# Other fixed sums, a different split of the gather work and an earlier load of v in the expert stage of a decoder layer

## The chip, the core and the metric

The kernel runs on one core of a Trainium2 chip. The metric is device time in microseconds (us), from the start of the program to its end, lower is better. The core's engines each work through their own queue of instructions in a fixed order: TensorE (PE in the profile; PEld is its weight load), VectorE (DVE), ScalarE (ACT), GpSimd (POOL) and SyncE (SP). SP issues most of the transfers; POOL issues the gathers. An instruction whose inputs or buffer aren't ready holds up everything behind it on its engine.

## The reference, cut to what matters

```python
# x: 1024 tokens x 1024; two norm/mix layers come first, then PEER:
q = (xb @ w_query).reshape(T, 8, 2, 128)
s = einsum('thpk,hpnk->thpn', q, sub_keys)        # 8 heads, 2 x 128 keys
...                                               # top 16 of 16 x 16 pairs per head
idx = ...                                         # 128 of 16384 experts for each token
gate = softmax(best_s)
u, v = expert_u[idx], expert_v[idx]               # rows of 1024
act = gelu(einsum('td,thkd->thk', xb, u))
out = einsum('thk,thkd->td', gate * act, v)
```

Each token uses 128 of 16384 experts. The kernel computes this in two ways. For 352 tokens it gathers the 128 rows of u and the 128 rows of v that a token names (the gather way). For the other 672 tokens it multiplies with all 16384 experts, densely, and weighs the result with a gate matrix that is zero where an expert was not chosen (the dense way).

## The kernel before

The change concerns the last stage alone, from about 1260 us to the end. It walks over 128 blocks of 128 experts. All matrix products are done with split operands: an f32 matrix is kept as a high half (name ending in h) and a remainder (l), and a product is three matmuls, high by high, high by remainder, remainder by high. A split is an ACT copy to the high half (line 115) and a DVE subtraction for the remainder (line 116).

For each block `b`:

- `u_steps(b)` (line 1155) is the **first product**: the block's u (`wh`, `wl`, fetched as `in_uT` by SP at line 203) times the 672 dense tokens, in two column parts of 384 and 288 (`SPL`), 24 matmuls each, into two PSUM banks named `pa`. A Gelu on ACT (line 1168) empties each bank into a tile `Wl`. For 40 blocks (`EARLIES`, every third one) this was done in an earlier stage; the result is loaded from memory instead (`Wl<-ged`, line 1450).
- `w_step(b)` (line 1382) multiplies by the gates on DVE (line 1384) and splits the result into `Wh`, `Wl`.
- `v_load(b)` (line 1387) loads the block's v (`vl<-in_v`, line 1389) and splits it into `vh`, `vl`.

After every third block `v_phase` (line 1392) does the **second product** of three earlier blocks: for each of the two column parts j and each of the eight slices c of the 1024 output columns, nine matmuls (3 blocks by 3). There are 16 such sums per phase. Twelve go to a PSUM bank, alternately `pa` (the two banks that the first product also uses) and `pv` (two more), and DVE then adds them to `acc` tiles (line 1419). Four of them, the pairs (j, c) in `FIXED`, have a bank of their own (`pacc`) for the whole stage and are not added up in between.

One **group** of work is therefore: two first products (call them u A and u B), one loaded block, and one phase; 96 + 144 = 240 matmuls. The phase that follows u B works on the blocks up to u A, so u B's result is not needed at once.

The gather way runs beside it, as background work: POOL issues one gather of 128 rows per step (line 1084, five row buffers), DVE multiplies and sums u rows (line 1102) or adds v rows (line 1094). `along(columns)` releases as many background steps as the matmul columns just issued have earned. The order of instructions on each engine is then settled by a scheduler when the kernel is built: it ranks instructions by their place in the program and moves up what it holds to be ready.

Of the kernel before, what the change touches and what calls it, by code (L numbers as in the profile page):

```python
# [19 lines left out]
P = 128  # L20
S = 1024
DM = 1024
# [8 lines left out]
NK = 128  # L31
# [19 lines left out]
EARLY = 40  # L51
EARLIES = [b for b in range(NK) if b % 3 == 1][:EARLY]
SLOTS = SB + 1
ROWS = 4
TB = 8
NE = 3.6
NF = 2.1 * TG / 64
MID = 1
WL = 3
WS = SLOTS + 2  # L60
VS = SLOTS + 2
WB = 2
WJ = 0
PAIRS = [(0, 2), (2, 4)]
FIXED = [(0, 1), (0, 5), (1, 1), (1, 5)]
RB = 0.15
RD = 0.0
DG = 2
# [31 lines left out]
def build(tc, A, out, dbg=None):  # L100
    nc = tc.nc
    V, C, G, T, SY = nc.vector, nc.scalar, nc.gpsimd, nc.tensor, nc.sync
    dbg = dbg or {}

    def pool(st, name, bufs=1, side="left", space=None):
        kw = {} if space is None else {"space": space}
        if space is DRAM:
            return st.enter_context(tc.tile_pool(name=name, bufs=bufs, **kw))
        if space is PSUM:
            return st.enter_context(tc.tile_pool(name=name, bufs=bufs, reuse_waits="tile", **kw))  # L110
        return st.enter_context(tc.tile_pool(name=name, bufs=bufs, side=side, reuse_waits="tile", **kw))

    def split(hi, lo, src):

        C.activation(hi, src, AF.Copy)  # L115
        V.tensor_tensor(lo, src, hi.bitcast(F32), op=OP.subtract)  # L116

    def raw_tile(pl, shape, name, lb):

        return pl.tile(shape, F32R, name=name + "l", bufs=lb).bitcast(F32)  # L120

    def halves_of(pl, raw, shape, name, lb, hb):
        hi = pl.tile(shape, F32R, name=name + "h", bufs=hb)
        lo = pl.tile(shape, F32R, name=name + "l", bufs=lb)
        split(hi, lo, raw)
        return hi, lo
# [15 lines left out]
    with root:  # L142
# [29 lines left out]
        def advance(cost):  # L172
            if bg["back"] is None:
                return
            bg["due"] += cost
            while bg["spent"] < bg["due"]:
                bg["spent"] += next(bg["back"], 1e9)
# [826 lines left out]
        def norm_store(pl, o, w, parts, fw, r, sq):  # L1004

            sf = pl.tile([P, 4], F32, name="sf", bufs=3)[:w]
            for j in range(2):
                C.activation(sq[:w], parts[j], AF.Square, accum_out=sf[:, j:j + 1])
            V.scalar_tensor_tensor(sf[:, 0:1], sf[:, 0:1], DM * EPS, sf[:, 1:2], op0=OP.add, op1=OP.add)
            rsqrt(sf[:, 2:3], sf[:, 0:1], sf[:, 3:4], 5)  # L1010
            for j in range(2):
                sl = slice(j * 512, j * 512 + 512)
                V.scalar_tensor_tensor(r[:w, sl], parts[j], sf[:, 2:3], fw[:w, sl], op0=OP.mult, op1=OP.mult)
            SY.dma_start(out[o:o + w], r[:w])
# [165 lines left out]
        def u_early(blocks, rate):  # L1180

            left = blocks * 3.0 * KC * TD
            while left > 0:
                c = next(early, None)
                if c is None:
                    return False
                left -= c
                advance(c / 2400.0 * RATES[rate])
            return True
# [33 lines left out]
        def early_along(steps_):  # L1223
            for c in steps_:
                fill[0] += c * NE / 26.0
                if fill[0] - fill[1] > 0.25:
# [16 lines left out]
        for g in range(FULL, NG):  # L1243
            o, w = GG[g]
            r = slice(P - REST + o, P - REST + o + w)
            n = steps[g]
# [42 lines left out]
        def gates(t):  # L1289
# [3 lines left out]
            for q4 in range(w // TG):  # L1293
# [17 lines left out]
                for qb in range(TG // TB):  # L1311
# [24 lines left out]
                    advance(TB * 0.107 * RATES["F"])  # L1336
                    u_early(NF * TB / TG, "F")
                SY.dma_start(gd[:, :, (t * P) // TG + q4].rearrange("g p b t -> p g b t"),
# [4 lines left out]
        while u_early(1.0, "G"):  # L1343
# [5 lines left out]
        mp = pool(stM, "mp")  # L1349
        psM = pool(stM, "psM", space=PSUM)  # L1350
        accs = {(j, c): mp.tile([P, n], F32, name=f"acc{j}{c}") for j, (_, n) in enumerate(SPL) for c in range(KC)
                if (j, c) not in FIXED}
        fixed = {f: psM.tile([P, 512], F32, name=f"pacc{f[0]}{f[1]}", bufs=1) for f in FIXED}

        turn = [0]

        def new_pv():

            turn[0] ^= 1
            if turn[0]:  # L1360
                return psU.tile([P, 512], F32, name="pa", bufs=2)
            return psM.tile([P, 512], F32, name="pv", bufs=2)
# [8 lines left out]
        def along(columns):  # L1371
            advance(columns * per_column)
# [3 lines left out]
        Vs = {}  # L1376

        def g_load(q):
            gs[q] = mp.tile([P, NTG, GB, TG], F32, name="gsb", bufs=2)
            SY.dma_start(gs[q], gd[q])  # L1380
# [4 lines left out]
            Ws[b] = halves_of(mp, ge, [P, TD], "W", WS, SLOTS)  # L1385

        def v_load(b):
            raw = raw_tile(mp, [P, DM], "v", VS)
            SY.dma_start(raw, A["v"][b * P:(b + 1) * P])
            Vs[b] = halves_of(mp, raw, [P, DM], "v", VS, SLOTS)  # L1390

        def v_phase(b0, b1):
            last = b1 == NK
            for j, (o, n) in enumerate(SPL):
                for c in range(KC):
                    fx = (j, c) in fixed
                    pv = fixed[j, c] if fx else new_pv()
                    i = 0
                    for b in range(b0, b1):
                        wh, wl = Ws[b]  # L1400
                        vh, vl = Vs[b]
                        for l, r in ((vh, wh), (vl, wh), (vh, wl)):
                            T.matmul(pv[:, :n], l[:, c * P:(c + 1) * P], r[:, o:o + n],  # L1403
                                     start=(i == 0 and (not fx or b0 == 0)),
                                     stop=(i == 3 * (b1 - b0) - 1 and (not fx or last)))
                            i += 1
                    if last and fx:
                        accs[j, c] = raw_tile(mp, [P, TD], "W", WS)[:, :n]
                    a = accs.get((j, c))
                    if last and fx:  # L1410
                        C.activation(a, pv[:, :n], AF.Copy, scale=modc[:, 5, c:c + 1])
                    elif last:
                        V.scalar_tensor_tensor(a, pv[:, :n], modc[:, 5, c:c + 1], a, op0=OP.mult, op1=OP.add)
                    elif fx:
                        pass
                    elif b0 == 0:
                        V.tensor_copy(a, pv[:, :n])
                    else:
                        V.tensor_tensor(a, a, pv[:, :n], op=OP.add)  # L1419
                    if not last:  # L1420
                        along(3.0 * (b1 - b0) * n)
                if last:
                    for t in range(o // P, -(-(o + n) // P)):
                        w = WT[t]
                        parts = []
                        for q in range(2):
                            pt = new_pv()[:w]
                            for c in range(4):
                                cs_ = slice((q * 4 + c) * P, (q * 4 + c + 1) * P)
                                d = pt[:, c * P:(c + 1) * P]  # L1430
                                if j:
                                    T.matmul(d, ident[:w, :w], x1s[t][:w, cs_], start=True, stop=False)
                                    T.matmul(d, accs[j, q * 4 + c][:, t * P - o:t * P - o + w], ident, start=False, stop=True)
                                else:
                                    T.transpose(d, accs[j, q * 4 + c][:, t * P - o:t * P - o + w], ident)
                            if j == 0:
                                sl = slice(q * 512, (q + 1) * 512)
                                V.tensor_tensor(rs[t][:w, sl], pt, x1s[t][:w, sl], op=OP.add)
                                pt = rs[t][:w, sl]
                            parts.append(pt)  # L1440
                        norm_store(mp, REST + t * P, w, parts, fw, rs[t], sq)
# [3 lines left out]
        for b in range(NK):  # L1445
            if b % GB == 0 and b + GB < NK:
                g_load(b // GB + 1)
            if b in EARLIES:
                ge = raw_tile(mp, [P, TD], "W", WS)
                SY.dma_start(ge, ged[EARLIES.index(b)])  # L1450
            else:
                ge = raw_tile(mp, [P, TD], "W", WS)
                for c in u_steps(b, ge):
                    along(c)
            w_step(b, ge)
            v_load(b)
            if b - prev == SB:
                v_phase(prev, prev + SB)
                prev += SB
        for _ in bg["back"] or ():  # L1460
            pass
        while NK - prev > SB:
            v_phase(prev, prev + SB)
            prev += SB
# [5 lines left out]
        for t in range(DT):  # L1470
            n = ("wl", "wh")[t % 2] if t < 5 else "vl"
# [69 lines left out]
```

## Time and profile before

| | |
|---|---|
| median of 3 runs | 2999.6 us (2998.78 to 3002.16) |
| the profiled execution | 2986.61 us, span 2984.8 us |
| mean granted TensorE clock | 0.981 of full speed |
| PE busy / DVE busy over the span | 95% / 85% |
| ACT busy / POOL busy over the span | 31% / 29% |
| the stage that is changed | about 1260 to 2964 us |

Busy shares are unions of the recorded instructions. "Idle before" an instruction is put down to what released it. A wait on PE counts only while nothing runs on it; the first matmuls after a wait can also be slower.

### The profile page before, as it was taken

How to read it: one execution, taken by the hardware profiler on the slowest of the kernel's cores; microseconds unless marked ns; L12 is line 12 of the kernel's file. 1: busy time of each engine (PE TensorE's matmuls, PEld its weight loads, DVE VectorE, ACT ScalarE, POOL GpSimd, SP SyncE). 2: the span in 40 equal slices, each digit the busy share in tenths (PEclk: the TensorE clock that was granted, in tenths of full speed). 3: DMA queues.
4: the chain of work that ended last, by engine and by line, in shares of the span. 5: the costliest groups of instructions: out<-in, count | busy, mean ns of one | idle time of the engine just before them, and what ended most of it. 6: DMA issues, size and time to landing. Idle time of an engine off the chain costs nothing.

```text
span 2984.8 us, 47174 instructions
## 1 busy us (share of the span) xinstructions
PE 2850.0 (95%) x18190; PEld 2687.0 (90%) x18190; DVE 2547.3 (85%) x5369; ACT 939.3 (31%) x1548; POOL 862.6 (29%) x726
## 2 busy tenths in 40 slices
PE   8999999989999999999999999999899999899998
PEld 6887898878999889999999999999899999899998
DVE  6885549988999987488999989889899988899998
ACT  5643645333222455422222222222222222222222
POOL 0000000000000000045554544445454554555451
PEclk9999999989999999999999999999999999999999
DMA  7424342244223687788889989899899998899995
GB/s 271 146 90 140 127 155 64 78 141 146 70 90 112 212 253 244 246 307 323 324 324 330 340 321 340 325 323 332 304 351 327 329 324 316 311 327 329 324 320 182
DMA packets 288676, 740.01 MB, mean 248 GB/s; under 512 B 27873, under 2 KB 122081, under 8 KB 282050
## 3 DMA queue, kind: packets, MB, share of 16 engines
q0 software_dynamic: 102944, 374.78, 35.3%
q1 hardware_dynamic: 185506, 362.22, 35.3%
q8 instruction: 142, 2.33, 0.3%
q14 instruction: 84, 0.69, 0.1%
HBM read 666.29 MB, written 70.52 MB: 247 GB/s over the span
## 4 chain that ended last, share of the span: by engine, by line
issue 27%; DVE 25%; DMA 20%; PE 20%; POOL 5%; ACT 2%; SPq 0%; DVEq 0%; POOLq 0%; ACTq 0%
PE pp L469 5%; DVE gacc L1094 5%; DMA wl<-in_uT 3%; DVE wl L116 3%; DVE acc L1419 3%; DMA Wl<-ged 2%; PE pq L875 2%; PE pp L875 2%; DVE vl L116 2%; DVE Wl L1384 1%; DMA more<-in_u,idx 1%; PE pa L1163 1%; PE ps L579 1%; PE pp L380 1%; POOL more L1084 1%
## 5 line engine op out<-in xcount | busy, mean ns | idle before, releaser
L1163 PE MATMUL pa<-h2h,wh 128*128 128x384 f32 (+1 forms) x1840 | 590.3, 321 | 14.2 <-DVE acc L1419 12.0
L1163 PE MATMUL pa<-h2l,wh 128*128 128x384 f32 (+1 forms) x1840 | 588.0, 320 | 0.0
L1163 PE MATMUL pa<-h2h,wl 128*128 128x384 f32 (+1 forms) x1840 | 584.0, 317 | 2.7 <-DVE wl L116 2.7
L1163 PEld LDWEIGHTS pa<-h2h,wh 128*128 128x128 f32 x1840 | 347.9, 189 | 19.4 <-DVE acc L1419 13.3
L1163 PEld LDWEIGHTS pa<-h2h,wl 128*128 128x128 f32 x1840 | 349.0, 190 | 2.9 <-DVE wl L116 2.9
L1163 PEld LDWEIGHTS pa<-h2l,wh 128*128 128x128 f32 x1840 | 349.7, 190 | 0.0
L115 ACT ACTIVATE Wh<-Wl 128x672 fp32r<-128x672 f32 x128 | 98.0, 766 | 754.4 <-PE pv L1403 487.9
L115 ACT ACTIVATE wh<-wl 128x1024 fp32r<-128x1024 f32 x187 | 197.7, 1057 | 385.6 <-DMA wl<-in_uT 187.1
L1403 PE MATMUL pa<-Wh,vh 128*128 128x384 f32 (+1 forms) x768 | 251.5, 327 | 53.6 <-ACT Wl L1168 41.7
L116 DVE TENSOR_TENSOR wl<-wl,wh 128x1024 fp32r<-128x1024 f32 x187 | 228.0, 1219 | 75.3 <-ACT wh L115 74.6
L1403 PE MATMUL pv<-Wh,vh 128*128 128x384 f32 (+1 forms) x768 | 245.4, 320 | 5.2 <-DVE acc L1419 4.9
L1403 PE MATMUL pa<-Wl,vh 128*128 128x384 f32 (+1 forms) x768 | 245.8, 320 | 0.7 <-DVE Wl L116 0.7
L1403 PE MATMUL pa<-Wh,vl 128*128 128x384 f32 (+1 forms) x768 | 245.6, 320 | 0.0
L1403 PE MATMUL pv<-Wh,vl 128*128 128x384 f32 (+1 forms) x768 | 243.7, 317 | 0.0
L1403 PE MATMUL pv<-Wl,vh 128*128 128x384 f32 (+1 forms) x768 | 243.3, 317 | 0.0
L1403 PEld LDWEIGHTS pa<-Wh,vh 128*128 128x128 f32 x768 | 145.7, 190 | 67.7 <-ACT Wl L1168 52.1
L115 ACT ACTIVATE vh<-vl 128x1024 fp32r<-128x1024 f32 x128 | 134.4, 1050 | 125.5 <-DMA vl<-in_v 75.5
L1403 PE MATMUL pacc<-Wh,vh 128*128 128x384 f32 (+1 forms) x512 | 163.6, 320 | 1.5 <-ACT vh L115 1.5
L1403 PE MATMUL pacc<-Wh,vl 128*128 128x384 f32 (+1 forms) x512 | 163.7, 320 | 0.6 <-DVE vl L116 0.6
L1403 PE MATMUL pacc<-Wl,vh 128*128 128x384 f32 (+1 forms) x512 | 163.0, 318 | 0.0
L116 DVE TENSOR_TENSOR vl<-vl,vh 128x1024 fp32r<-128x1024 f32 x128 | 155.7, 1217 | 3.2 <-ACT vh L115 3.2
L469 PE MATMUL pp<-h1h,wh 128*128 128x512 f32 x384 | 157.3, 410 | 0.0
(1944 smaller groups left out, 7405.8 us busy)
## 6 DMA issues: line engine op xcount, KB each, us to landing
wl<-in_uT SPq DMA_DIRECT2D x128, 512.0 KB, 5.9
vl<-in_v SPq DMA_DIRECT2D x128, 512.0 KB, 7.9
gd<-stg SPq DMA_DIRECT2D x21, 2048.0 KB, 9.3
gsb<-gd SPq DMA_DIRECT2D x32, 1344.0 KB, 9.1
wl<-in_win SPq DMA_DIRECT2D x48, 512.0 KB, 3.5
wa<-in_wada SPq DMA_DIRECT2D x16, 1024.0 KB, 5.0
wl<-in_wq SPq DMA_DIRECT2D x32, 512.0 KB, 3.5
ged<-ge SPq DMA_DIRECT2D x40, 336.0 KB, 3.1
```

The source lines that it names most:

```text
L115: C.activation(hi, src, AF.Copy)
L116: V.tensor_tensor(lo, src, hi.bitcast(F32), op=OP.subtract)
L380: T.matmul(pvs[t], l[:, t * P:(t + 1) * P], r, start=(k == 0 and l is h1[0][k] and r is wi[0]), stop=(k == KC - 1 and l is h1[1][k]))
L469: T.matmul(pp, l[:, k], r[k], start=(i == 0), stop=(i == 3 * KC - 1))
L579: T.matmul(ps_[:, c], X[:, cs_], Y[:, cs_], start=True, stop=True)
L875: T.matmul(pq[:, :m], l[:, k], hs[k, r][:, o:o + m], start=(i == 0), stop=(i == 3 * KC - 1))
L1084: G.indirect_dma_start(out=r, out_offset=None, in_=src, in_offset=IndirectOffsetOnAxis(ap=idx[:n, s0 + j:s0 + j + 1], axis=0))
L1094: V.scalar_tensor_tensor(ac, r, aw[:, j:j + 1], ac, op0=OP.mult, op1=OP.add))
L1163: T.matmul(pa[:, :n], l[:, k], h2[k, r][:, o:o + n], start=(i == 0), stop=(i == 3 * KC - 1))
L1384: V.tensor_tensor(gv, gv, gs[b // GB][:, :, b % GB], op=OP.mult)
L1403: T.matmul(pv[:, :n], l[:, c * P:(c + 1) * P], r[:, o:o + n], start=(i == 0 and (not fx or b0 == 0)), stop=(i == 3 * (b1 - b0) - 1 and (no ...
L1419: V.tensor_tensor(a, a, pv[:, :n], op=OP.add)
```

## The change

Three edits. `FIXED`, the four sums with a bank of their own, are no longer c = 1 and 5 of each column part but the first two sums of a phase and its last two; `turn` starts the alternation so that a phase's first shared sum goes to `pv`. The background steps earned beside the first product are halved (`AU`), and those beside the second product raised so that the total stays (`AV`). v is loaded by SP ahead of its block's first product, and split where it was loaded and split before.

```diff
+AU = 0.5
+AV = 1.0 + (1.0 - AU) * (NK - EARLY) / NK
...
-FIXED = [(0, 1), (0, 5), (1, 1), (1, 5)]
+FIXED = [(0, 0), (0, 1), (1, 6), (1, 7)]
...
-        turn = [0]
+        turn = [1]
...
         def v_load(b):
-            raw = raw_tile(mp, [P, DM], "v", VS)
-            SY.dma_start(raw, A["v"][b * P:(b + 1) * P])
-            Vs[b] = halves_of(mp, raw, [P, DM], "v", VS, SLOTS)
+            Vs[b] = raw_tile(mp, [P, DM], "v", VS)
+            SY.dma_start(Vs[b], A["v"][b * P:(b + 1) * P])
+
+        def v_split(b):
+            Vs[b] = halves_of(mp, Vs[b], [P, DM], "v", VS, SLOTS)
...
-                        along(3.0 * (b1 - b0) * n)
+                        along(AV * 3.0 * (b1 - b0) * n)
...
+            v_load(b)
             if b in EARLIES:
...
                 for c in u_steps(b, ge):
-                    along(c)
+                    along(AU * c)
             w_step(b, ge)
-            v_load(b)
+            v_split(b)
```

What this does to the order on three engines follows. The new kernel's line numbers are 3 to 6 higher (1163 is 1166, 1403 is 1408, 115 is 118, 1168 is 1171, 203 is 206, 1389 is 1392, 1450 is 1456).

PE, before, at the end of u B and the start of a phase (`h2` is the dense tokens' matrix):

```order
L1163 MATMUL pa<-h2h_86,wh 128x288
L1163 MATMUL pa<-h2l_87,wh 128x288
L1163 MATMUL pa<-h2h_86,wl 128x288
L1403 MATMUL pa<-Wh,vh 128x384
L1403 MATMUL pa<-Wh,vl 128x384
L1403 MATMUL pa<-Wl,vh 128x384
```

PE, after, at the same place of a group; `pacc_13127` and `pacc_13128` are the sums (0, 0) and (0, 1), and the first matmuls of the former have been done earlier:

```order
L1166 MATMUL pa<-h2h_86,wl 128x288
L1408 MATMUL pacc_13127<-Wh,vh 128x384
L1408 MATMUL pacc_13127<-Wh,vl 128x384
L1408 MATMUL pacc_13127<-Wl,vh 128x384
L1408 MATMUL pacc_13128<-Wh,vh 128x384
L1408 MATMUL pacc_13128<-Wh,vl 128x384
L1408 MATMUL pacc_13128<-Wl,vh 128x384
```

The phase no longer begins in `pa`: after u B come 3 to 18 matmuls into fixed banks, then nine into `pv`, then the first into `pa`. And between u A and u B, after:

```order
L1166 MATMUL pa<-h2h_86,wl 128x288
L1166 MATMUL pa<-h2h_72,wh 128x384
L1166 MATMUL pa<-h2l_73,wh 128x384
L1408 MATMUL pacc_13127<-Wh,vh 128x384
L1166 MATMUL pa<-h2h_72,wh 128x288
L1166 MATMUL pa<-h2l_73,wh 128x288
L1408 MATMUL pacc_13127<-Wh,vl 128x384
L1408 MATMUL pacc_13127<-Wl,vh 128x384
```

In 27 of the groups the second column part of u B now starts three to five matmuls after u A's end (24 before), in the bank that u A has just filled.

ACT, before, from u A's second Gelu to u B's second Gelu and on (128x384 and 128x288 out of `pa` are the Gelus of the two column parts; `wh<-wl` is the high half of a later block's u):

```order
L1168 ACTIVATE Wl<-pa 128x288
L115 ACTIVATE Wh<-Wl 128x672
L115 ACTIVATE vh<-vl 128x1024
L1168 ACTIVATE Wl<-pa 128x384
L115 ACTIVATE wh<-wl 128x1024
L1168 ACTIVATE Wl<-pa 128x288
L115 ACTIVATE Wh<-Wl 128x672 x2
```

ACT, after, from u A's second Gelu to u B's second Gelu and on:

```order
L1171 ACTIVATE Wl<-pa 128x288
L118 ACTIVATE vh<-vl 128x1024
L118 ACTIVATE Wh<-Wl 128x672
L118 ACTIVATE wh<-wl 128x1024
L1171 ACTIVATE Wl<-pa 128x384
L118 ACTIVATE vh<-vl 128x1024
L1171 ACTIVATE Wl<-pa 128x288
L118 ACTIVATE wh<-wl 128x1024
```

A u copy stood between u B's two Gelus and stands behind both of them now; another one, of the next group's u A, stands between u A's second Gelu and u B's first. In some groups that one also stands ahead of `Wh<-Wl`.

SP, before, one group's transfers, with the engines or transfers that an issue waits for in brackets:

```order
L1389 DMA vl<-in_v 128x1024 [waits DMAHW6_49,PE_49]
L1389 DMA vl<-in_v 128x1024 [waits PE_49]
L203 DMA wl<-in_uT 128x1024 [waits DMAHW5_49,DVE_49]
...
L1389 DMA vl<-in_v 128x1024 [waits DMAHW6_49,DMAHW4_49]
L1450 DMA Wl<-ged 128x672 [waits Activation_49]
L203 DMA wl<-in_uT 128x1024 [waits DMAHW0_49,DVE_49]
```

SP, after:

```order
L1392 DMA vl<-in_v 128x1024 [waits PE_49]
L206 DMA wl<-in_uT 128x1024 [waits DMAHW0_49,PE_49]
L1392 DMA vl<-in_v 128x1024
L206 DMA wl<-in_uT 128x1024 [waits DMAHW2_49,DMAHW0_49,DVE_49]
L1392 DMA vl<-in_v 128x1024 [waits DMAHW7_49,DMAHW3_49]
L1456 DMA Wl<-ged 128x672 [waits DMAHW4_49,DVE_49]
```

One fetch of u per group now waits for PE: for u A's last matmuls, whose buffer it takes. The second v load of a group has moved behind it.

## Rows read from the trace of the kernel before

**Rows 1.** The page, busy time of each engine over the span.

```profile
PE 2850.0 (95%) x18190; PEld 2687.0 (90%) x18190; DVE 2547.3 (85%) x5369; ACT 939.3 (31%) x1548; POOL 862.6 (29%) x726
```

**Rows 2.** Windows: three fast groups, two slow ones, the stretch of 39 groups.

```profile
core 0: us, PE busy (x) PEld busy (x) DVE busy (x) ACT busy (x) POOL busy (x), PEclk, DMA share, GB/s
1295.70:1332.70 37.00, 37.00 (x243) 37.00 (x242) 33.66 (x55) 8.76 (x14) 21.89 (x18) 1.00 0.93 343
...
1607.60:1648.20 40.60, 38.72 (x242) 38.48 (x242) 36.81 (x52) 8.95 (x15) 19.84 (x18) 0.96 0.90 324
...
1770.90:1807.90 37.00, 37.00 (x243) 37.00 (x242) 35.41 (x48) 9.00 (x15) 19.14 (x18) 1.00 0.96 358
...
2124.30:2170.10 45.80, 39.72 (x243) 39.40 (x242) 37.79 (x52) 8.85 (x14) 21.89 (x19) 0.93 0.85 301
2170.10:2207.10 37.00, 37.00 (x242) 37.00 (x242) 34.97 (x48) 8.82 (x14) 19.80 (x17) 1.00 0.96 357
...
1295.70:2847.40 1551.70, 1479.76 (x9367) 1458.24 (x9366) 1391.37 (x1946) 348.97 (x491) 795.61 (x656) 0.99 0.91 327
```

**Rows 3.** PE's waits in these 39 groups: us, times, longest.

```profile
PE pa L1403 <- ACT Wl L1168: 41.3, 33, 3.0
PE pa L1163 <- DVE acc L1419: 12.0, 4, 6.1
PE pa L1403 <- DVE acc L1419: 11.6, 11, 2.4
PE pv L1403 <- DVE acc L1419: 4.9, 9, 1.5
```

**Rows 4.** ACT's and DVE's waits in the same groups.

```profile
ACT wh L115 <- DMA wl<-in_uT: 130.5, 35, 5.7
...
DVE Wl L1384 <- DMA Wl<-ged: 18.8, 9, 4.7
DVE Wl L1384 <- ACT Wl L1168: 17.6, 12, 2.8
...
DVE wl L116 <- ACT wh L115: 10.2, 7, 2.1
DVE Wl L116 <- ACT Wh L115: 6.9, 6, 2.2
```

**Rows 5.** Timeline around one start of a phase: start us, length, engine, instruction [idle before].

```profile
1505.86 1.22 DVE L116 TENSOR_TENSOR wl<-wl,wh 128x1024 fp32r<-128x1024 f32 x1
...
1506.20 0.29 PE L1163 MATMUL pa<-h2h,wl 128*128 128x288 f32 x1
...
1507.10 0.33 SPq L203 DMA_DIRECT2D wl<-in_uT  x1
...
1512.87 1.06 ACT L115 ACTIVATE wh<-wl 128x1024 fp32r<-128x1024 f32 x1 [4.81 <-DMA wl<-in_uT]
...
1513.83 0.39 ACT L1168 ACTIVATE Wl<-pa 128x288 f32<-128x288 f32 x1
...
1514.28 0.44 PE L1403 MATMUL pa<-Wh,vh 128*128 128x384 f32 x1 [1.17 <-ACT Wl L1168]
```

**Rows 6.** DVE's groups by line in the 39 groups: busy us, mean ns, idle before.

```profile
L116 DVE TENSOR_TENSOR vl<-vl,vh 128x1024 fp32r<-128x1024 f32 x117 | 142.3, 1216 | 0.0
L1419 DVE TENSOR_TENSOR acc<-acc,pa 128x384 f32<-128x384 f32 (+1 forms) x233 | 115.6, 496 | 1.1 <-PE pa L1403 1.1
...
L116 DVE TENSOR_TENSOR Wl<-Wl,Wh 128x672 fp32r<-128x672 f32 x117 | 99.9, 854 | 6.9 <-ACT Wh L115 6.9
L1384 DVE TENSOR_TENSOR Wl<-Wl,gsb 128x672 f32<-128x672 f32 x116 | 98.9, 853 | 36.6 <-DMA Wl<-ged 18.8 <-ACT Wl L1168 17.6
...
L1094 DVE SCALAR_TENSOR_TENSOR gacc<-more,aw,gacc 128x1024 f32<-128x1024 f32 x64 | 81.8, 1278 | 5.6 <-DMA more<-in_v,idx 5.3
```

**Rows 7.** Transfers, issue to landing: the v load's median, then wl's extremes.

```profile
vl<-in_v SPq DMA_DIRECT2D x118, 512.0 KB, 7.9
...
DMA to landing us min/median/max: 3.4/6.4/10.9
```

**Rows 8.** A ten-microsecond window with a long wait of PE.

```profile
2130.00:2140.00 10.00, 5.27 (x22) 5.27 (x23) 6.88 (x10) 1.06 (x1) 2.26 (x3) 0.67 0.70 246
```

## The prediction

> **What bounds the kernel now.** The page's first part comes first: PE is busy for 95% of the span, DVE for 85%, ACT and POOL for about 30% [rows 1]. These are averages over several stages, so the next view is windows of single groups within the last stage [rows 2]. Three groups of 240 matmuls take 37.0 us each with no gap on PE: that is the pace which PE alone allows, 37.0 / 240 = 0.154 us a matmul. In those same groups DVE is busy for 33.7 to 35.4 us and the DMA engines for 93 to 96%, so all other engines can carry that pace. Other groups need 40.6 or 45.8 us. From 1295.7 to 2847.4 us there are 9367 recorded matmuls, 39 groups; they take 1551.7 us, 39.8 each. At 37.0 they would take 1443.0, so 108.7 us lie above PE's own pace: that is the most that the change can win here. Of it 1551.7 - 1479.8 = 71.9 us are idle time of PE. The other 36.8 come with the idle time: in a ten-microsecond window around a wait of 6.1 us the granted clock is 0.67 of full speed, a mixture of the 2.4 and the 1.2 GHz level, and PE does 22 matmuls [rows 8]. I charge them to the waits in proportion: a microsecond of PE's wait costs 108.7 / 71.9 = 1.51 us.
>
> PE's waits say whom it waits for [rows 3]. 33 times, 41.3 us in all, the first matmul into `pa` of a phase waits for a Gelu on ACT. Three rows, 12.0 + 11.6 + 4.9 = 28.5 us, are a bank which DVE has not yet added to `acc`. With the factor these are 62.4 and 43.0 us.
>
> The timeline of one such start shows how the Gelu comes to be late [rows 5]. A u fetch takes the buffer of an earlier u, so SP issues it only when DVE's subtraction of that one ends (1505.86 + 1.22 = 1507.08, issue at 1507.10). The data come 5.8 us later. ACT's copy of them stands ahead of u B's second Gelu, and waits 4.81 us. The Gelu ends at 1514.22, and PE's first `pa` matmul of the phase, which needs the bank, has waited 1.17 us. ACT lost 130.5 us in this way over the stretch [rows 4].
>
> DVE's rows name what it waited for: results from memory 18.8, Gelus 17.6, ACT's copies of u 10.2 and of W 6.9 [rows 4]. It was busy 1391.4 us, 35.7 a group, and idle 160.3, 4.1 a group. What those four rows leave, 106.8 us or 2.7 a group, is in small pieces before many rows, for the most part before gather steps whose rows had not landed, as in the last group of [rows 6].
>
> **The change part by part.**
>
> *Fixed sums at the ends, first shared sum in `pv`.* After u B come 3 to 18 matmuls into fixed banks and nine into `pv` before `pa` is needed, where there was nothing. That is 12 to 27 matmuls, 1.85 to 4.2 us, against waits of 41.3 / 33 = 1.25 us on average and 3.0 at the longest [rows 3]. Besides, the copy that held up the Gelu stands behind it now. All of the wait goes: **-62.4 us**; bounds 0 and -62.4. The work added is nothing: as many sums as before go to DVE. In 27 groups u B's second column part starts three to five matmuls after u A's end, in the bank just filled: a matmul (0.29) and a Gelu (0.39) [rows 5] against three times 0.154, so at most 0.2 to 0.3 us each, 8 us in all. I cost this at nothing, since ACT stands waiting there.
>
> *The new fetch of u behind PE.* This is what is late next. The fetch for the next group's u A now takes u A's own buffer and is issued when u A ends on PE. It lands 6.4 us later at the median, 3.4 to 10.9 at the extremes [rows 7], and ACT's copy takes 1.06 [rows 5]: DVE can start its subtraction 7.5 us after u A's end. That copy stands ahead of u B's first Gelu, which is then done at 7.9; its bank is needed 48 + 12 to 27 matmuls after u A's end, at 9.2 to 11.6 us. So PE is covered at the median; with the slowest landing (12.4) it would wait 0.8 to 3.2 us. On DVE less lies in between: two gather rows (2 x 1.28), a gate product (0.85), and the subtractions of v (1.22) and W (0.85) [rows 6], 5.5 us. So DVE gets a wait that it hadn't: 2.0 us a group, 78 us in all, if it is on time; 4.5 if the two rows are done already; 6.5 with the slowest landing; nothing if it runs that much behind, as it may in a group where it is the slow engine. The nearest row: of 130.5 us of late copies only 10.2 reached DVE, 8% [rows 4]. 8% of what ACT will wait here (6.4 less two copies, 4.3 us, times 39 = 168) would be 13 us. DVE's subtraction stands closer behind the copy than before, so I take more: 0.6 us a group, **+23.4 us**, bounds 0 and +78.
>
> *The waits on DVE that go.* u B's Gelus are no longer held up, and results from memory are asked for a phase earlier: 17.6 + 18.8 = 36.4 us of DVE's idle time, 0.9 a group. Some of it comes back as time in which DVE catches up, and PE's wait for DVE shrinks. I take half of the 43.0: **-21.5 us**, bounds 0 and -43.0.
>
> *Half the gather share beside the first product.* The total of gather steps stays. In the order of DVE, 9 or 10 of a group's rows stand between the evictions of the phase, before and after the change, so I cost it at nothing. The cover is the slack of banks: three products of nine matmuls, 4.2 us, against three rows in one place, 3.8 us. If the cover is gone, a group loses a few tenths, as in the rows of late `acc`.
>
> *v asked for ahead.* Two of a group's three loads were already issued at the end of a phase, and a load takes 7.9 us [rows 7] of a group's 39.8: nothing, in either direction. What it changes is SP's queue, where the second v now stands behind the u fetch and so behind PE's end of u A. It lands at 7.9 us, and the second Gelu of u B behind its copy is ready at 7.9 + 1.06 + 0.39 = 9.4; the second use of `pa` comes 18 matmuls after the first, at 12.0 us or later.
>
> A rule speaks against this part's order. The Trainium skill, "DMA: Bandwidth & Descriptors", section "Issuing engines are not separate DMA queues", says that transfers run on the same 16 DMA engines and interleave, whoever started them. By it, to stand ahead of v on SP gives the u fetch no precedence. The trace agrees as far as a fetch of u takes 3.4 to 10.9 us for the same 512 KB [rows 7]; it has no pair issued in this order. The time would be that of the fifth rival, instead of the 2939 below.
>
> **The sum.** -62.4 - 21.5 + 23.4 = -60.5 us in the 39 groups; the three groups outside them and the other stages I leave as they are. The profiled execution takes 2986.6 us, the median of three runs is 0.44% more, 2999.6. So 2986.6 - 60.5 = 2926.1, and times 1.0044 **2939 us**, 38.2 us a group. A check from DVE's side: 34.7 to 35.7 busy and 2.7 of waits for rows make 37.4 to 38.4.
>
> **The rivals.**
> 1. *Full pace.* All of PE's waits go and the new fetch is hidden: 37.0 a group, 2986.6 - 108.7 = 2877.9, **2891 us**. For it: three groups already ran like this. Against it: DVE's 35.7 busy leave 1.3 a group for waits, and those for rows alone are 2.7 now.
> 2. *DVE and its rows are the bound.* 35.7 + 2.7 = 38.4 us, and half of the new wait, 1.0, on top: 39.4, 39 x 39.4 = 1536.6, that is -15.1 and **2985 us**. PE then waits for DVE where it waited for ACT. For it: the waits for rows stand outside this change, and the DMA engines are at 91%. Against it: one of the fast groups needed only 33.7 us of DVE.
> 3. *Slower: the fetch behind PE.* The new wait of 2.0 us hits DVE whole: 38.4 + 2.0 = 40.4 a group, 39 x 0.6 = +23, **3023 us**. It decides from 39.8 - 38.4 = 1.4 us a group of the new wait that nothing absorbs. For it: transfers of up to 10.9 us, and the DMA load. Against it: the 8% of before.
> 4. *The Gelu wait stays,* because u B's Gelu is now behind the new copy. Half of the 62.4 back would give 2970; I count this among the cases of the second rival.
> 5. *Slower still: the fetch shares with v.* The second v is issued right behind the fetch. If the fetch then takes v's 7.9 us [rows 7] instead of 6.4, DVE's new wait is 3.5 us; whole, that is 41.9 a group, 39 x 2.1 = +82, **3082 us**. For it: DMA engines that are busy for 91%. Against it: the median over all fetches of u, which have v's loads beside them too, is 6.4.
>
> **How the numbers follow.** The forecast (2915 to 2965) gets 0.50, full pace 0.13, the second rival with the fourth 0.20, the third 0.13 and the fifth 0.04. A measurement here can tell about 0.2%, 6 us, from no change: below 2994 is faster, above 3006 slower. The second rival's cases lie on both sides of the first bound, 0.11 faster and 0.09 the same. That makes faster 0.74, same 0.09, slower 0.17. The range goes from 2885, just below full pace, to 3012, which leaves out some 0.03 below and 0.13 above.
>
> **What would show it.** Right: PE's `pa` waits for Gelu at the start of a phase are gone, DVE's waits for results from memory and for Gelus with them, and what DVE waits for ACT's `wh` copy is about 0.6 us a group, at a pace of 38.2. Wrong: that wait is above 1.4 us a group, or DVE is busy for more than 0.92 of the stretch with PE waiting for `acc`, or the waits before gather rows grow above 2.7 us a group because the rows now come in another place. If `pa` still waits for the Gelu, the count of matmuls ahead of it was not the cover that I took it for.

## The result and the profile after

The changed kernel takes 3014.3 us (median of 5, 3001.4 to 3020.0), the kernel before 2999.6 (median of 5); the ratio is 1.0051, interval 1.0027 to 1.0075. It is slower by 0.5%, where 2% faster was forecast, and 2 us above the upper end of the range. The profiled execution of the changed kernel takes 3001.4 us, span 2999.5. Both profiled executions lie 13 us below their medians. Executions of one kernel differ by up to 1%, so below the waits are read from the profiles, and the size of an effect from the ratios.

The same 39 groups, from the first row of [rows 2] on, are now at 1293.8 to 2860.9 us. Windows of that stretch and of one slow group, columns as in [rows 2]:

```profile
1647.92:1687.51 39.59, 38.35 (x244) 37.06 (x242) 34.42 (x49) 9.59 (x14) 21.47 (x17) 1.00 0.89 319
1293.80:2860.90 1567.10, 1499.05 (x9372) 1455.67 (x9371) 1391.93 (x1956) 353.76 (x491) 827.21 (x658) 0.99 0.90 324
```

1567.1 us are 40.2 a group, 15.4 more in all than before. PE's waits in the stretch, answering to [rows 3]:

```profile
PE pa L1408 <- DVE acc L1424: 27.0, 30, 4.6
PE pv L1408 <- DVE acc L1424: 16.1, 26, 2.2
PE pacc L1408 <- ACT Wh L118: 6.3, 5, 2.0
PE pa L1166 <- ACT Wl L1171: 5.5, 6, 2.5
PE pacc L1408 <- ACT vh L118: 2.7, 3, 1.6
```

The 33 waits of a phase's first `pa` for a Gelu, 41.3 us, are gone. In their place are waits for DVE's evictions, 43.1 us (28.5 before), short ones for halves that are needed earlier, and 5.5 us in which the first product waits for a Gelu. PE's idle time is 1567.1 - 1499.05 = 68.05 us, 3.9 less than before, although the stretch is longer. The weight loads tell why: PEld is busy for nearly the same time as before (1455.7, 1458.2), so its idle time grew from 93.5 to 111.4 us. Its waits in the changed kernel:

```profile
PEld pa L1408 <- DVE acc L1424: 38.5, 44, 5.0
PEld pv L1408 <- DVE acc L1424: 28.6, 44, 2.5
PEld pa L1166 <- ACT Wl L1171: 13.4, 29, 2.7
```

Matmuls overlap: in this trace they start 0.17 us apart and are shown as 0.34 us long. So a wait shorter than a running matmul makes PE late without making it idle. 88 waits for evictions are counted here, 56 on PE. In the slow group above PE's idle is 1.24 us, the clock is granted in full, and yet the group takes 2.6 us more than 37.0; the weight loads' idle time in it is 39.59 - 37.06 = 2.5 us.

DVE's and ACT's waits, answering to [rows 4]:

```profile
DVE wl L119 <- ACT wh L118: 49.9, 18, 4.8
DVE vl L119 <- ACT vh L118: 36.3, 10, 5.2
DVE Wl L119 <- ACT Wh L118: 16.9, 13, 4.5
DVE Wl L1387 <- ACT Wl L1171: 5.9, 6, 2.7
...
ACT wh L118 <- DMA wl<-in_uT: 134.8, 51, 6.3
```

DVE's busy time didn't change (1391.4, now 1391.9), so its idle time, 160.3 before and 175.2 now, holds the difference of the two stretches, and its rows divide it: late copies of u +39.7, of v +36.3 (none before), of W +10.0; results from memory -18.8, Gelus -11.7; and what is left, mostly gather rows, fell from 106.8 to 66.2, -40.6. Together +14.9.

One such wait in the timeline of the changed kernel (start us, length, engine, instruction, idle before):

```profile
1655.20 0.29 PE L1166 MATMUL pa<-h2h,wl 128*128 128x288 f32 x1
...
1655.53 0.33 SPq L206 DMA_DIRECT2D wl<-in_uT  x1
...
1655.75 1.21 DVE L1105 SCALAR_TENSOR_TENSOR grow__17065<-grow__17065,hx 128x1024 f32<-128x1024 f32 x1
...
1655.90 0.43 SPq L1392 DMA_DIRECT2D vl<-in_v  x1
...
1656.90 0.85 DVE L1387 TENSOR_TENSOR Wl<-Wl,gsb 128x672 f32<-128x672 f32 x1
1657.67 1.21 DVE L119 TENSOR_TENSOR vl<-vl,vh 128x1024 fp32r<-128x1024 f32 x1
1658.81 0.84 DVE L119 TENSOR_TENSOR Wl<-Wl,Wh 128x672 fp32r<-128x672 f32 x1
1659.57 1.27 DVE L1097 SCALAR_TENSOR_TENSOR gacc<-grow__17114,aw,gacc 128x1024 f32<-128x1024 f32 x1
...
1664.44 1.06 ACT L118 ACTIVATE wh<-wl 128x1024 fp32r<-128x1024 f32 x1 [3.35 <-DMA wl<-in_uT]
1665.54 1.23 DVE L119 TENSOR_TENSOR wl<-wl,wh 128x1024 fp32r<-128x1024 f32 x1 [4.69 <-ACT wh L118]
...
1666.99 1.07 ACT L118 ACTIVATE vh<-vl 128x1024 fp32r<-128x1024 f32 x1 [1.19 <-DMA vl<-in_v]
...
1672.84 0.55 DVE L1424 TENSOR_TENSOR acc<-acc,pv 128x384 f32<-128x384 f32 x1
...
1673.44 0.45 PE L1408 MATMUL pv<-Wh,vh 128*128 128x384 f32 x1 [0.81 <-DVE acc L1424]
```

u A ends on PE, SP issues the fetch, and it lands 8.9 us later. DVE has five instructions in the meantime, those that the prediction counted (two rows, gate product, two subtractions), then waits for 4.69 us. From 1665.54 on it never stops, but its first eviction comes 0.8 us after PE needs the bank. v's load was issued 0.37 us behind this fetch, which took 8.9 us against a median of 6.4 before [rows 7]; v itself took 11.1 us against 7.9. The Trainium skill, "DMA: Bandwidth & Descriptors", section "Issuing engines are not separate DMA queues", has transfers interleave whoever issued them; this one pair agrees, as being ahead on SP didn't make the fetch quick. No run here separates the two.

### The profile page after: what moved, and what is told of

Same layout as the page of the kernel before. It is cut to its first block, busy times and chain, and to the rows that moved or that the text cites. A ratio compares the mean times of both kernels' runs of the same rounds, so it can differ in the third digit from the quotient of the medians.

```text
span 2999.5 us, 47065 instructions
## 1 busy us (share of the span) xinstructions
PE 2864.9 (96%) x18190; PEld 2681.6 (89%) x18190; DVE 2543.7 (85%) x5369; ACT 942.9 (31%) x1548; POOL 889.9 (30%) x726
## 4 chain that ended last, share of the span: by engine, by line
PE 37%; DVE 27%; DMA 17%; issue 11%; POOL 5%; ACT 3%; SPq 0%; DVEq 0%; POOLq 0%; ACTq 0%
PE pa L1166 13%; DMA wl<-in_uT 6%; PE pp L472 5%; DVE gacc L1097 3%; PE pa L1408 3%; PE pv L1408 3%; DVE wl L119 3%; PE pacc L1408 3%; DMA vl<-in_v 2%; PE pg L1333 2%; DVE acc L1424 2%; PE pp L878 2%; DVE s L929 1%; PE ps L582 1%; ACT wh L118 1%
## 5 line engine op out<-in xcount | busy, mean ns | idle before, releaser
L1408 PE MATMUL pacc<-Wh,vh 128*128 128x384 f32 (+1 forms) x512 | 163.8, 321 | 10.7 <-ACT Wh L118 6.3
L1408 PEld LDWEIGHTS pv<-Wh,vh 128*128 128x128 f32 x768 | 145.9, 190 | 31.3 <-DVE acc L1424 29.6
```

## Experiments

Each was measured beside the kernel before on the same chip; ratios are to it. The names of lines are those of each kernel.

**e1, the fixed sums alone.**

```diff
-FIXED = [(0, 1), (0, 5), (1, 1), (1, 5)]
+FIXED = [(0, 0), (0, 1), (1, 6), (1, 7)]
-        turn = [0]
+        turn = [1]
```

> The four fixed sums at the phase's ends and the turn alone; gather share and v as before. No u fetch waits for PE in this order. Theory 1 (the halved gather share brought the fetch behind PE, and the fixed sums pay as forecast): PE's waits of pa for a Gelu at a phase's start are gone (41.3 us before) and nothing takes their place, 2940 to 2960 us. Theory 2 (rival: with the fixed sums at the ends twelve evictions stand in a row, DVE falls behind them, and PE's waits for acc take the place): waits for acc about 43 us as in the changed kernel instead of 28.5, 3000 to 3015 us.

Measured: 2964.4 us, ratio 0.986 (0.9832 to 0.9887). PE's waits in its 39 groups:

```profile
PE pv L1403 <- DVE acc L1419: 23.1, 23, 3.9
PE pa L1403 <- DVE acc L1419: 7.8, 17, 2.1
PE pacc L1403 <- DVE Wl L116: 7.1, 7, 1.7
...
PE pa L1163 <- DVE acc L1419: 0.3, 1, 0.3
```

This edit pays 1.4%, about 42 us. The time is 4 us above theory 1's range, since something did take the place of the Gelu waits: 7.1 us of waits for W's remainder, needed earlier by the fixed sums. The Gelu waits are gone; waits for `acc` stay at 31.2 (28.5 before), against theory 2.

**e2, the halved gather share alone.**

```diff
+AU = 0.5
+AV = 1.0 + (1.0 - AU) * (NK - EARLY) / NK
-                        along(3.0 * (b1 - b0) * n)
+                        along(AV * 3.0 * (b1 - b0) * n)
-                    along(c)
+                    along(AU * c)
```

> The halved gather share alone; fixed sums and v as before. 23 of the last 80 or so u fetches wait for PE in this order (37 in the changed kernel, none before). Theory 1: slower than before, as DVE waits for ACT's wh or vh copies behind these fetches; 86 us of such waits in the changed kernel times 23/37 is 53 us, 3020 to 3050 us. Theory 2: no change, 2994 to 3006 us.

Measured: 3041.2 us, ratio 1.0124 (1.0097 to 1.0152). DVE's two longest waits, and PE's two:

```profile
DVE wl L119 <- ACT wh L118: 70.9, 28, 5.9
DVE vl L119 <- ACT vh L118: 24.1, 11, 5.7
...
PE pa L1166 <- ACT Wl L1171: 32.8, 19, 3.1
PE pa L1166 <- DVE wl L119: 18.2, 18, 2.3
```

The share that the prediction priced at nothing costs about 37 us by itself, within theory 1's range, and brings both late copies with it, without the early load of v. PE then waits in the first product, for u's remainder and for Gelus; its waits for `acc` are 25.4 us, 28.5 before.

**e3, the changed kernel with a share of 0.6.**

```diff
-AU = 0.5
+AU = 0.6
```

> The changed kernel with the gather share 0.6 instead of 0.5; in this order no u fetch waits for PE. Theory 1: DVE's waits for wh and vh copies fall from 86 us to about 10 as before, 2940 to 2960 us. Theory 2: waits for acc as in the changed kernel, 3000 to 3015 us.

Measured: 2973.1 us, ratio 0.9891 (0.9864 to 0.9918). DVE's waits:

```profile
DVE vl L119 <- ACT vh L118: 34.4, 12, 4.7
DVE Wl L1387 <- ACT Wl L1171: 28.3, 23, 2.5
DVE wl L119 <- ACT wh L118: 10.4, 10, 1.7
```

A step of a tenth in the share is worth 1.6%. Waits for u's copies fell as expected; those for v's didn't, so theory 1's sum of the two at 10 was wrong, and the time lies between both ranges.

**e4, the early load of v alone.** The edit of `v_load` and `v_split` as in the change, nothing else.

> v loaded ahead of the first product alone. The order differs from before in a handful of SP's rows and nowhere else. Both theories: no change, 2994 to 3006 us.

Measured: 2997.8 us, ratio 0.998 (0.996 to 1.000): no effect that can be told.

**e5, every second u fetch in a tile of its own.** With a fourth tile beside the three that exist, a fetch can be issued about a group earlier.

```diff
+        for i in range(2, NK - EARLY, 2):
+            own[len(order) - NK + EARLY + i] = mp
-                raws[n] = raw_tile(up, [P, KC, P], "w", WL)
+                raws[n] = raw_tile(own[n], [P, KC, P], "wo", 1) if n in own else raw_tile(up, [P, KC, P], "w", WL)
```

> The changed kernel, but every second fetch of u goes into a tile of its own (4 KB a partition more), so that it can be issued about a group earlier; gather share 0.5, fixed sums and v as in the changed kernel. 34 u fetches still wait for PE in this order, but all have more than 7.5 us of DVE work between their release and their subtraction (in the changed kernel 29 have less). Theory A (what costs is that DVE reaches the subtraction before fetch and copy are done): DVE's waits for wh fall from 50 us to under 10, 2955 to 2980 us. Theory B (what costs is a fetch queued behind PE on SP): as the changed kernel, 3005 to 3020 us.

Measured: 2980.5 us, ratio 0.9923 (0.9898 to 0.9949), half a microsecond above theory A's range. DVE's waits:

```profile
DVE vl L119 <- ACT vh L118: 51.1, 20, 5.3
DVE wl L119 <- ACT wh L118: 25.6, 10, 5.7
```

With everything else of the change in place, an earlier fetch pays 1.3%. The waits for u's copies halved, not to under 10; those for v's grew.

**e6, every u fetch in one tile of its own.** As e5 with `range(2, NK - EARLY)`.

> The changed kernel, but every fetch of u goes into one tile of its own, the remainders keep the three others: no fetch waits for PE, each waits for the DVE subtraction before it. 34 of them have less than 7.5 us of DVE work ahead of their subtraction, 61 us short in all by count. Theory A: as slow as the changed kernel or slower, 3005 to 3040 us, DVE waits for wh of 40 us or more. Theory B: 2955 to 2980 us.

Measured: 3021.9 us, ratio 1.0063 (1.0040 to 1.0085). DVE's waits:

```profile
DVE wl L119 <- ACT wh L118: 78.5, 29, 6.2
DVE vl L119 <- ACT vh L118: 32.6, 10, 5.4
```

No fetch waits for PE, and DVE waits longer for u than in the changed kernel. e5 and e6 decide against theory B: in e5 some fetches still wait for PE and the kernel is faster, in e6 none does and it is as slow as the changed kernel. A fetch behind PE is no cost by itself; what e5 has and e6 lacks is a fetch that starts long before DVE needs it: from issue to subtraction DVE works 31.9 us at the median in e5, 10.1 in e6.

**e7, the fixed sums with the tile of e5.** Share and v as before.

> The fixed sums alone as in e1, with every second fetch of u in a tile of its own. Theory A: as e1 or a little faster, since DVE's waits for wh were 7 us there: 2950 to 2968 us. Theory B: 34 fetches now wait for PE, 2990 to 3020 us.

Measured: 2937.7 us, ratio 0.978 (0.9751 to 0.981), better than either theory said. Its stretch, and PE's waits:

```profile
1292.45:2796.04 1503.59, 1470.02 (x9366) 1448.09 (x9365) 1389.65 (x1946) 350.19 (x491) 825.58 (x655) 1.00 0.92 337
```

```profile
PE pv L1405 <- DVE acc L1421: 11.1, 19, 2.0
PE pacc L1405 <- DVE Wl L116: 8.5, 8, 1.7
PE pa L1405 <- DVE acc L1421: 8.0, 15, 2.3
```

38.6 us a group. No wait of ACT or DVE for u is left, DVE's idle time is 113.9 us, and PE's waits for `acc` fell to 19.1. Against e1 the tile pays 0.8% (0.978 / 0.986), where the share is whole and DVE's waits for u's copies were only 6.8 us: ACT's copies no longer wait for the fetch (161 us in e1), and with that 15.4 us of DVE's waits for Gelus are gone. So the 1.3% of e5 can't all be a cost of the share given back. With the tile in both, the share of e5 still costs 0.9923 / 0.978 = 1.015; without it, by e8 below, 1.019, and the intervals don't tell these two apart.

**e8, fixed sums and share, without the early v.** The diffs of e1 and e2 together.

> Fixed sums and halved gather share, v as before. If the parts add up (ratios 0.986 and 1.0124, v none): 0.998, about 3000 us. If the early load of v matters in this order, where it did not alone: 2980 to 2990 us, and v is then worth the 0.5 to 0.9% by which the changed kernel is slower than this.

Measured: 3019.1 us, ratio 1.0050 (1.0028 to 1.0072), the same as the changed kernel. So v adds nothing here either, and the parts don't add up: 0.986 x 1.0124 = 0.998. On top of the fixed sums the share costs 1.0050 / 0.986 = 1.019.

**e9, the turn alone.** The last two lines of e1's diff.

> The kernel before with the turn alone: the phase's first shared sum goes to pv, so that 18 matmuls (nine into pv, nine into the fixed sum c = 1) stand ahead of the first pa instead of none; fixed sums, gather share and v as before. Theory A (the cover ahead of pa is what pays in the fixed-sums edit): PE's waits of pa for a Gelu fall from 41 us to under 8, and the time is that of e1, 2955 to 2975 us. Rival (the place of the fixed sums pays or costs by itself, through DVE's evictions): 2935 to 2950 if twelve evictions in a row cost, 2980 to 2995 if the place pays.

Measured: 3007.3 us, ratio 1.0029 (1.0010 to 1.0047), outside all three ranges. PE's waits:

```profile
PE pa L1163 <- DVE acc L1419: 50.9, 27, 8.3
PE pv L1403 <- DVE acc L1419: 9.9, 14, 2.6
PE pa L1403 <- DVE acc L1419: 7.8, 14, 2.4
PE pa L1403 <- ACT Wl L1168: 6.2, 6, 2.5
```

The Gelu waits fell from 41.3 to 6.2 us, as the cover ahead of `pa` should make them, and nothing was won: u A's two column parts now wait for evictions, 50.9 us against 12.0, 41.1 of them ahead of the second part. A phase has twelve shared sums; begun in `pv` it ends in `pa`, and the next first product needs that bank at once.

**e10, the place of the fixed sums alone.** The first two lines of e1's diff.

> The four fixed sums at the phase's ends without the turn: 18 matmuls into fixed banks stand ahead of the first pa (27 in e1). Theory A: as e1, 2955 to 2975 us. Rival: if 18 matmuls are too few as a cover, waits of pa for a Gelu of 10 us or more remain, 2975 to 2990 us.

Measured: 2962.6 us, ratio 0.9882 (0.9858 to 0.9906), like e1. PE's waits:

```profile
PE pa L1403 <- DVE acc L1419: 22.7, 26, 4.7
PE pv L1403 <- DVE acc L1419: 7.6, 24, 1.6
...
PE pa L1403 <- ACT Wl L1168: 2.0, 4, 0.9
```

The waits at both ends are gone but for 2.0 us: two fixed sums at the start cover the Gelu, two at the end the last evictions, for which u A's matmuls no longer wait (12.0 us before). The turn adds nothing that can be told.

**e11 and e12, the changed kernel with the tile of e5 and a share of 1.25 and 0.75.**

```diff
-AU = 0.5
+AU = 1.25
```

> As e5 (fixed sums, v ahead, every second u in a tile of its own) but with the gather share beside the first product at 1.25 instead of 0.5, that beside the second at 0.83. Theory A: more rows stand ahead of the subtractions and fewer between the evictions: at least as fast as e7 (share 1), 2925 to 2940 us. Rival (the share of 1 is the balance, rows now delay DVE's gate products): 2945 to 2970 us.

> As e11 with a gather share of 0.75 (1.17 beside the second product). Theory A: between e5 (0.5, ratio 0.992) and e7 (1, ratio 0.978): 2945 to 2965 us. Rival (only the fetch of u counts, which has the same lead as in e7): 2935 to 2942 us.

Measured: 2978.1 us, ratio 0.9925 (0.9898 to 0.9951) at 1.25, and 2933.7, ratio 0.978 (0.9754 to 0.9806) at 0.75. Both go against theory A and past the rivals' ranges by a little: with the fetch out of the way shares of 0.75 and 1 (e7) are the same, and more than that costs again. DVE's two longest named waits at 1.25:

```profile
DVE Wl L1389 <- DMA Wl<-ged: 24.1, 9, 4.9
DVE more L1105 <- DMA more<-in_u,idx: 14.5, 9, 5.4
```

and at 0.75 its waits for copies:

```profile
DVE vl L119 <- ACT vh L118: 4.3, 3, 3.1
DVE wl L119 <- ACT wh L118: 2.7, 2, 2.3
```

e7 and e12 beat the kernel before by 2.2%, with intervals from 1.9 to 2.5%.

## Why the prediction was wrong

**The step that failed** is "Half the gather share beside the first product", of which the prediction says "I cost it at nothing". By e2 it costs 1.2% alone, and by e1 and e8 1.9% with the fixed sums, which is more than they bring. The prediction looked at the rows that stand between evictions, whose number hardly changed. It didn't look at the rows that left the first product: they were the work with which DVE passed the time between a u fetch's release and its subtraction. In the trace before, DVE is busy for 6.0 us at least between SP's issue of a fetch and that subtraction, and for 15.9 at the median of 83 fetches; in the changed kernel 20 of 83 have less than 6.0, the least 2.8, and the median is 9.9. The timelines show the same from ACT's side: from SP's issue to ACT's copy passed 9.8 us at the median before, 6.3 after, which is what a landing takes, and 29.6 in e7.

That this is how the share costs is read from waits. Among the kernels with the fixed sums, DVE's late copies of u, v and W and the time rise together: 0 and 7 us at a ratio of 0.978 (e7, e12), 7 at 0.986 (e1), 48 at 0.989 (e3), 87 at 0.992 (e5), 103 at 1.005 (the changed kernel), 118 at 1.005 and 1.006 (e8, e6). e11, slower without late copies, has another cost. A rival is the other half of the move, more rows between the evictions. Their number hardly changed from before to the changed kernel (10.0 and 9.6 a phase, counted in the traces), but only because two edits cancel: the fixed sums alone leave 6.8 (e1), the share alone makes 12.4 (e2). In e2 PE doesn't wait longer for `acc`, and e5, e6, e8 and the changed kernel all have 9.5 or 9.6 at times that differ by 1.4%, so this rival can't be the whole. On top of the fixed sums PE's waits for `acc` rise with the share, from 31.2 us in e1 to 48.6 in e8, and no run tells how much of that is rows and how much late copies.

**The new fetch, +23.4 us.** The wait was found, with its place and its five instructions, but taken as 0.6 us a group. It measured 39.7 / 39 = 1.0 for u, and with the late copies of v and W 86.0 / 39 = 2.2. The row chosen as nearest, 8% of ACT's late copies, came from an order in which DVE had more work ahead (15.9 against 9.9 us at the median). The waits for v's copies weren't foreseen: the text asked whether v's landing covers a Gelu on PE, not what DVE does meanwhile. And its cause was put on PE's end, which e5 and e6 refute: e2 has it by the share alone, while in e1, without the share, u's late copies are 6.8 us.

**Fixed sums, -62.4 us.** The mechanism was right in that the named waits went to nothing in the changed kernel and in e1. But the reason given, matmuls ahead of the first `pa`, is half of it: e9 has that cover and wins nothing, since the turn leaves the last shared sum in `pa`; e1, which is e9 with the sums moved, has the two fixed sums behind it, and u A's wait of 50.9 us falls to 0.3. What the edit is worth, 42 us in e1, is below the term: waits for halves came in, and those for `acc` didn't fall. The bank just filled, put at nothing and 8 us at most, shows in the weight loads alone: 19 of them wait for its Gelu, 5.6 us in all.

**Half of DVE's late evictions, -21.5 us.** Wrong in sign: those waits grew from 28.5 to 43.1 us. The timeline shows one way, a DVE that waits beside the first product and starts the evictions late; but e1, with few late copies, has 31.2 too, so the half wasn't there to win. That results from memory and Gelus would no longer hold DVE came true (-30.5 of 36.4 us), but not for the reason given: with the fixed sums alone 33.8 us of them stay (e1), with the share alone 10.7 (e2). The share replaced them by other waits, and 86.0 came back.

**v ahead at nothing** held (e4, e8). **Waits for gather rows at 2.7 a group** did not: 1.7, probably since rows land while DVE waits for something else.

**The rivals.** The third, the wait that hits DVE whole (3023 us, chance 0.13), comes nearest in time, with 40.4 us a group against 40.2, and that is in part luck: u's wait was 1.0 us a group more, not 2.0, and the sign that the prediction named, more than 1.4, was passed only together with the waits for v's and W's copies, at 2.2. Nor did it hit DVE whole: 1.0 us a group of waits for rows went, and DVE's idle time grew by 0.4. The fifth rival (3082) did not come: the time stayed below it, though the fetch in the timeline took 8.9 us.

**Open:** why v's copies come late at shares of 0.5 and 0.6 in every variant (24 to 51 us) and hardly at 0.75. The traces show two things: DVE has less work between v's issue and its subtraction (11.8 us at the median, 17.1 before), and v lands later, for where ACT waited for it 19 of 29 loads took over 10 us in the changed kernel, none of 36 before. No run gave v another buffer, so the two aren't separated. Why 1.25 is slower than 1 is read from waits only. That one microsecond of PE's wait costs 1.51 did not carry over: 1567.1 - 1443.0 = 124.1 above PE's pace to 68.1 idle is 1.82.

## What to carry to other kernels

Background work that is "only moved" is also cover: before moving it, add up, on each engine that works in order, the work between a transfer's release and the first instruction that needs its data, and compare that with the upper end of the landing times. Moving it changes the rows between evictions as well, so count both places. When a bank is handed from one product to another, look at both ends of the sequence; covering one end by turning the alternation moves the wait to the other. Where matmuls overlap, read the waits of the weight loads beside those of PE, since short waits show there alone.

## What was not expected of the hardware

PE's idle time fell by 3.9 us while the same matmuls took 15.4 us longer: waits under a running matmul are not idle time of PE. A lower clock isn't behind it: the granted clock is 0.99 in both stretches, and the weight loads, which last 0.19 us at full clock and 0.33 in most of the window of [rows 8] with its 0.67, were busy 2.6 us less.
